# Fourteen pairs of up products instead of twelve in a two-layer hybrid decoder trunk

## The chip, the cores and the metric

The kernel runs on one core of one Trainium2 chip. The metric is the device time of one execution in microseconds (us); three executions are given by their median. Everything is float32 at the border; products on TensorE are made in three passes of a split format (below).

## The reference

Two layers, each with an RMS norm, one input projection, three kinds of mixing heads, an output projection, and an MLP. The change lies in the MLP alone:

```python
def rms_norm(x, g):
    y = x * lax.rsqrt(jnp.mean(x * x, axis=-1, keepdims=True) + NORM_EPS)
    return y * g
...
for l in range(DEPTH):                 # DEPTH = 2, SEQ = 512, D_MODEL = 1024, D_FF = 4096
    ...                                # mixing: x = x + mixed @ w_out[l]
    h = rms_norm(x, norm_mlp_g[l])
    x = x + jnp.square(jax.nn.relu(h @ w_mlp_up[l])) @ w_mlp_down[l]
return rms_norm(x, final_norm_g)
```

## The kernel before, in words

**Layout.** Everything is kept transposed: eight tiles `x[j]` of 128 features by 512 tokens. A weight group is 1024x128: eight blocks of 128x128, loaded as two halves of four blocks (256 KB each).

**Three passes.** Each product of a weight block and an activation block is three matmuls: high part by high part, high by low, low by high. So each weight half needs a cast to the high part on ScalarE (`whi`, L344) and a subtraction for the low part on VectorE (`wlo`, L345). The helper `weights()` hands out the halves from a ring of three buffers and one spare.

**The norm's factor late.** The up products take `x` times the norm weights (`acts`, tiles `ahif` and `alof`, eight each, L739 and L740); the factor of the norm per token (`rs`, tile `rsf`, copied at L771) is multiplied in afterwards, in `square()`: `r` = max(up, 0) times `rs` (VectorE, L1402), `m` = `r` squared (ScalarE, L1404), then `kept()` makes the split result `mh` (ScalarE, L1393) and `ml` (GpSimd, L1394), the "mids", in a ring of ten.

**Singles.** An up group made singly (`up(i)`) is 8 blocks x 3 passes = 24 matmuls of 512 columns. The first three (`NUP`) are issued in the hand-ordered stage of the layer (lists `ORDER`, run inside `manual_schedule`); the rest of the MLP is placed by the framework's scheduler, which gives each engine one fixed order.

**Pairs.** `two(i0, i1)` makes two up groups at once by a Strassen-Winograd scheme of 2x2 blocks: seven products (`p1` to `p7`) of four weight blocks each, 7 x 4 x 3 = 84 matmuls of 256 columns. It needs four sums of raw weights (`s1` to `s4`, VectorE, L1463), seven splits (`shi_p` on ScalarE L1457, `slo_p` on VectorE L1458), and, once for each layer, four kinds of block sums of the activations. Those are made in two steps: `bn[j]`, `x[j]` times the norm weights (ScalarE, L1429), which carries a bias `none` of zero whose only use is to order it after `rs`; and `blocks(k)`, which takes the pair `bn[k]`, `bn[k + 4]` and makes four half-width differences `t` (VectorE, L1435 to L1438), their high parts `thi` (ScalarE, L1442) and low parts `tlo` (VectorE, L1443). `p5`, `p6`, `p7` and `p4` each take one kind of sum of all four `k`. The tiles `bn[0..3]` and `bn[4..7]` share the two rings of five buffers (tags `shi`, `slo`) with the split sums of the pairs.

**Down.** `down(h, js)` adds to `x[j]` the product of the four mids 4h to 4h+3: 12 matmuls of 512 columns for each `j`, into one of two PSUM banks (tag `mm`), and one VectorE addition (L1518) that frees the bank.

**Order.** Eight singles, with `by_gain` and `blocks` issued after each of the last four; then `down(0)` for all eight `j`; then twelve pairs, each followed by half a down group as far as its mids are there. At the end of the second layer two pairs stand next to each other, and `last_group` makes the last down group and the final norm.

Of the kernel before, what the change touches and what calls it, by code (L numbers as in the profile page):

```python
# [10 lines left out]
F32 = mybir.dt.float32  # L11
# [12 lines left out]
P = 128  # L24
# [10 lines left out]
NG_IN = 26  # L35
# [140 lines left out]
         "wp/wlo 01201201201201202102102102102102102102102102102102102102102102102102102102 ")  # L176
NG = NG_IN + NG_OUT + NG_UP + NG_DN

N_ONE = 8

WHOLE = 5
PT = 1
# [86 lines left out]
def tile_trunk(ctx: ExitStack, tc: tile.TileContext, xT, wts, prm_d, cst_d, lora_d, gup_d, lam_d, fin_d, out):  # L269
# [299 lines left out]
    for l in range(L):  # L569
# [809 lines left out]
        with ExitStack() as mx:  # L1379
# [35 lines left out]

            bn, th = {}, {}
            none = cp.tile([P, NB], F32, tag="rr", bufs=2, name=f"none{l}")[:, :1]
            dve.tensor_scalar(none, rs[:, :1], 0.0, None, ALU.is_lt)  # L1420

            def by_gain(j):

                if j == 0:
                    fp.tile([P, 8], F32, tag="pad0", name=f"pad0_{l}")
                bn[j] = fp.tile([P, 2, H], F32, tag="shi" if j < 4 else "slo", bufs=5, name=f"bn{l}_{j}")
                if j == 4:
                    fp.tile([P, 24], F32, tag="pad1", name=f"pad1_{l}")
                act.activation(bn[j].rearrange("p a s -> p (a s)"), x[j], AF.Identity, scale=pr[:, C_GMLP + j:C_GMLP + j + 1],  # L1429
                               bias=none)  # L1430

            def blocks(k):
                b1, b2 = bn[k], bn[k + 4]
                t = [fp.tile([P, 2, H], F32, tag=f"s{2 * (k % 2) + i + 1}", name=f"t{l}_{k}_{i}") for i in range(2)]
                dve.tensor_tensor(t[0][:, 0], b1[:, 1], b1[:, 0], ALU.subtract)  # L1435
                dve.tensor_tensor(t[0][:, 1], b2[:, 1], t[0][:, 0], ALU.subtract)
                dve.tensor_tensor(t[1][:, 0], b2[:, 1], b1[:, 1], ALU.subtract)
                dve.tensor_tensor(t[1][:, 1], b2[:, 0], t[0][:, 1], ALU.subtract)  # L1438
                hi, lo = th[k] = [fp.tile([P, 4, H], F32R, tag=f"t{p}{k}", name=f"t{p}{l}_{k}") for p in ("hi", "lo")]
                for i in range(2):  # L1440
                    u = slice(2 * i, 2 * i + 2)
                    act.copy(hi[:, u], t[i])  # L1442
                    dve.tensor_tensor(lo[:, u], t[i], hi[:, u].bitcast(F32), ALU.subtract)  # L1443

            def two(i0, i1):

                n = f"{l}_{i0}"
                wg = wbase + NG_IN + NG_OUT

                def raw(i, a):  # L1450
                    t = fp.tile([P, 4, P], F32, tag="sraw", bufs=6, name=f"raw{n}_{i}_{a}")
                    nc.sync.dma_start(t.rearrange("p k c -> p (k c)"), wts[wg + i, :, a * P:(a + 4) * P])
                    return t

                def both(src, name):
                    hi, lo = [fp.tile([P, 4, P], F32R, tag=f"s{p}", bufs=5, name=f"s{p}{n}_{name}") for p in ("hi", "lo")]
                    act.copy(hi, src)  # L1457
                    dve.tensor_tensor(lo, src, hi.bitcast(F32), ALU.subtract)  # L1458
                    return hi, lo

                def sum_(name, a, b, op):
                    t = fp.tile([P, 4, P], F32, tag=name, name=f"{name}{n}")
                    dve.tensor_tensor(t, a, b, op)  # L1463
                    return t

                def small(name):
                    return fp.tile([P, H], F32, tag=name, bufs=2, name=f"{name}{n}")

                def product(pt, w, moving, first=True):

# [8 lines left out]
                smm = lambda q: lambda k: [p[:, q] for p in th[k]]  # L1479
# [24 lines left out]
                dve.tensor_tensor(c1, c1, p5, ALU.add)  # L1504
                s4 = sum_("s4", w12, s2, ALU.subtract)
                product(pb, both(s4, "p3"), blk(1, 1), False)
                dve.tensor_tensor(c0[:, H:], pb, u2, ALU.add)
                square([c0], f"{n}_0")
                product(pa, both(w22, "p4"), smm(3), False)
                square([pa, c1], f"{n}_1")  # L1510

            def down(h, js):

                g, k0 = h // 2, 4 * (h % 2)
                for j in js:
                    pt = psum("mm", 2, f"dn{l}_{h}_{j}")
                    mm3(pt, weights(wbase + NG_IN + NG_OUT + NG_UP + 8 * g + j, k0, k0 + 4), mids[4 * h:4 * h + 4], 4)
                    dve.tensor_tensor(x[j], pt, x[j], ALU.add)  # L1518
# [91 lines left out]
```

## Time and profile before

| what | value |
|---|---|
| median of 3 runs | 1241.13 us (1240.64 to 1241.17) |
| the profiled execution | 1241.0 us, its span 1239.2 us |
| TensorE matmul busy | 1227.2 us, 9572 matmuls |
| VectorE / ScalarE / GpSimd busy | 915.1 / 675.5 / 367.3 us |
| granted clock | 0.998 |

The span is the time from the first to the last instruction of the execution that was profiled. Busy times say how long an engine had at least one instruction in it; matmuls overlap (one of 512 columns shows 390 ns and the next starts 227 ns after it), so the pace of TensorE is read from the starts in the timeline and not from the durations. The first layer's MLP runs from about 279 us, the second layer's from about 889 us.

### The profile page before, as it was taken

How to read it: one execution, taken by the hardware profiler on the slowest of the kernel's cores; microseconds unless marked ns; L12 is line 12 of the kernel's file. 1: busy time of each engine (PE TensorE's matmuls, PEld its weight loads, DVE VectorE, ACT ScalarE, POOL GpSimd, SP SyncE). 2: the span in 40 equal slices, each digit the busy share in tenths (PEclk: the TensorE clock that was granted, in tenths of full speed). 3: DMA queues.
4: the chain of work that ended last, by engine and by line, in shares of the span. 5: the costliest groups of instructions: out<-in, count | busy, mean ns of one | idle time of the engine just before them, and what ended most of it. 6: DMA issues, size and time to landing. Idle time of an engine off the chain costs nothing.

```text
span 1239.2 us, 25134 instructions
## 1 busy us (share of the span) xinstructions
PE 1227.2 (99%) x9572; PEld 1050.8 (85%) x9572; DVE 915.1 (74%) x1776; ACT 675.5 (55%) x1410; POOL 367.3 (30%) x457
## 2 busy tenths in 40 slices
PE   9999999999999999999999999999999999999997
PEld 6788788888899998989888888888788999999987
DVE  6887888868767676765766777887686767676754
ACT  6785655548445454544565656564583545454543
POOL 2263637342311111120035454563231211111111
PEclk9999999999999999999999999999999999999999
DMA  6523333142433333321235243232433333323121
GB/s 216 164 88 98 108 92 111 53 154 85 136 102 96 108 95 103 102 85 44 69 104 167 82 131 111 88 84 71 152 103 121 101 102 102 103 95 109 53 68 69
DMA packets 84696, 127.92 MB, mean 103 GB/s; under 512 B 21472, under 2 KB 25568, under 8 KB 84576
## 3 DMA queue, kind: packets, MB, share of 16 engines
q1 hardware_dynamic: 83568, 125.64, 32.7%
q8 instruction: 75, 1.23, 0.4%
q10 hardware_dynamic: 1008, 0.68, 0.2%
q14 instruction: 45, 0.37, 0.1%
HBM read 117.11 MB, written 9.18 MB: 102 GB/s over the span
## 4 chain that ended last, share of the span: by engine, by line
PE 93%; DVE 2%; ACT 2%; POOL 1%; DMA 1%; issue 1%; ACTq 0%; POOLq 0%; DVEq 0%
PE dn L282 25%; PE pj L282 21%; PE pa L282 11%; PE po L282 8%; PE up L282 7%; PE pb L282 6%; PE dnF L282 4%; PE pc L282 3%; PE sc L282 1%; PE ptt L287 1%; PE pg L282 1%; DMA raw<-wts 1%; PE pyy L282 1%; PE pzw L282 1%; PE pst L282 1%
## 5 line engine op out<-in xcount | busy, mean ns | idle before, releaser
L1394 POOL TENSOR_TENSOR ml<-m,mh 128x512 fp32r<-128x512 f32 x64 | 108.9, 1716 | 480.9 <-ACT mh L1393 322.6
L344 ACT CAST whi<-raw 128x512 fp32r<-128x512 f32 x142 | 87.4, 619 | 162.1 <-PE dn L282 152.6
L282 PE MATMUL dn<-mh,whi 128*128 128x512 f32 x448 | 174.8, 390 | 0.0
L282 PE MATMUL dn<-ml,whi 128*128 128x512 f32 x448 | 174.6, 390 | 0.0
L282 PE MATMUL dn<-mh,wlo 128*128 128x512 f32 x448 | 174.5, 390 | 0.0
L683 POOL TENSOR_TENSOR wlo<-raw,whi 128x512 fp32r<-128x512 f32 x84 | 110.5, 1316 | 212.7 <-ACT whi L671 174.6
L282 PE MATMUL pj<-ahim,whi 128*128 128x512 f32 x392 | 156.8, 400 | 0.4 <-DVE vf L1280 0.4
L282 PE MATMUL pj<-ahim,wlo 128*128 128x512 f32 x392 | 156.5, 399 | 0.0
L282 PE MATMUL pj<-alom,whi 128*128 128x512 f32 x392 | 156.0, 398 | 0.0
L1518 DVE TENSOR_TENSOR x<-dn,x 128x512 f32<-128x512 f32 x112 | 77.3, 690 | 102.9 <-PE dn L282 102.9
L671 ACT CAST whi<-raw 128x512 fp32r<-128x512 f32 x142 | 87.7, 618 | 81.5 <-PE pj L282 27.6
L345 DVE TENSOR_TENSOR wlo<-raw,whi 128x512 fp32r<-128x512 f32 x142 | 115.2, 812 | 11.2 <-ACT whi L344 8.8
L282 PEld LDWEIGHTS dn<-mh,wlo 128*128 128x128 f32 x448 | 84.1, 188 | 17.8
L282 PEld LDWEIGHTS dn<-mh,whi 128*128 128x128 f32 x448 | 84.1, 188 | 17.5 <-issue 0.4
L282 PEld LDWEIGHTS dn<-ml,whi 128*128 128x128 f32 x448 | 84.1, 188 | 16.7
L1457 ACT CAST shi_p<-s 128x512 fp32r<-128x512 f32 x96 | 59.6, 621 | 70.0 <-PE pa L282 55.1
L282 PEld LDWEIGHTS pj<-ahim,whi 128*128 128x128 f32 x392 | 73.9, 188 | 14.1 <-issue 0.8
L282 PEld LDWEIGHTS pj<-alom,whi 128*128 128x128 f32 x392 | 73.9, 188 | 14.0 <-issue 0.5
L282 PEld LDWEIGHTS pj<-ahim,wlo 128*128 128x128 f32 x392 | 73.9, 188 | 13.9 <-issue 0.2
L1458 DVE TENSOR_TENSOR slo_p<-s,shi_p 128x512 fp32r<-128x512 f32 x96 | 68.0, 709 | 19.7 <-ACT shi_p L1457 17.2
L282 PE MATMUL pa<-tlo,shi_p 128*128 128x256 f32 x288 | 81.4, 282 | 0.0
L282 PE MATMUL pa<-thi,shi_p 128*128 128x256 f32 x288 | 81.2, 282 | 0.0
(414 smaller groups left out, 3202.4 us busy)
## 6 DMA issues: line engine op xcount, KB each, us to landing
raw<-wts SPq DMA_DIRECT2D x389, 256.0 KB, 2.7
qs<-dqhi SPq DMA_DIRECT2D x24, 128.0 KB, 3.7
ks<-dkhi SPq DMA_DIRECT2D x24, 128.0 KB, 3.7
x<-xT SPq DMA_DIRECT2D x8, 256.0 KB, 4.5
dqhi<-qhi SPq DMA_DIRECT2D x6, 256.0 KB, 3.3
dqlo<-qlo SPq DMA_DIRECT2D x6, 256.0 KB, 3.3
dkhi<-khi SPq DMA_DIRECT2D x6, 256.0 KB, 3.1
dklo<-klo SPq DMA_DIRECT2D x6, 256.0 KB, 3.5
```

The lines of the kernel that those rows point to most:

```text
L282: ins = nc.tensor.matmul(*a, **k)
L287: ins = nc.tensor.transpose(*a, **k)
L344: act.copy(hi[:, :n], raw[:, :n])
L345: (pool if a and lean[0] else dve).tensor_tensor(lo[:, :n], raw[:, :n], hi[:, :n].bitcast(F32), ALU.subtract)
L671: yield act.copy(hi[:, k0:k1], raw[:, k0:k1])
L683: yield eng.tensor_tensor(lo[:, k0:k1], raw[:, k0:k1], hi[:, k0:k1].bitcast(F32), ALU.subtract)
L1394: pool.tensor_tensor(lo, m, hi.bitcast(F32), ALU.subtract)
L1457: act.copy(hi, src)
L1458: dve.tensor_tensor(lo, src, hi.bitcast(F32), ALU.subtract)
L1518: dve.tensor_tensor(x[j], pt, x[j], ALU.add)
```

## The change

- Four up groups are made singly instead of eight (`N_ONE`), and fourteen pairs instead of twelve.
- `none` is made from the last low part of `acts` instead of `rs`, so that all `bn` depend on `x` and the norm weights only; the eight `by_gain` are issued together behind the four singles.
- `blocks` goes by kind of sum (`q`) and not by `k`: first the sums for `p5` of all `k`, then those for `p6`, `p7` and `p4`. The number of instructions is the same. It is issued behind the first half of `down(0)`.
- `down(0)` is made in two halves, the second behind the first pair. In the first, `j` = 0 and 1 open both banks together: three of the four mids for each, then the fourth for each.
- `s1` and `s3` of the first pair take `none` as an added scalar, and the copy of `p5` out of PSUM goes from VectorE to ScalarE.

```diff
-N_ONE = 8
+N_ONE = 4
...
-            dve.tensor_scalar(none, rs[:, :1], 0.0, None, ALU.is_lt)
+            dve.tensor_scalar(none, acts[NK - 1][1][:, :1].bitcast(F32), 0.0, None, ALU.mult)
...
-            def blocks(k):
-                b1, b2 = bn[k], bn[k + 4]
-                t = [fp.tile([P, 2, H], F32, tag=f"s{2 * (k % 2) + i + 1}", name=f"t{l}_{k}_{i}") for i in range(2)]
-                dve.tensor_tensor(t[0][:, 0], b1[:, 1], b1[:, 0], ALU.subtract)
-                dve.tensor_tensor(t[0][:, 1], b2[:, 1], t[0][:, 0], ALU.subtract)
-                dve.tensor_tensor(t[1][:, 0], b2[:, 1], b1[:, 1], ALU.subtract)
-                dve.tensor_tensor(t[1][:, 1], b2[:, 0], t[0][:, 1], ALU.subtract)
...
+            def blocks(q):
+                hi, lo = th[q] = [fp.tile([P, 4, H], F32R, tag=f"t{p}{q}", name=f"t{p}{l}_{q}") for p in ("hi", "lo")]
                 for i in range(2):
                     u = slice(2 * i, 2 * i + 2)
-                    act.copy(hi[:, u], t[i])
-                    dve.tensor_tensor(lo[:, u], t[i], hi[:, u].bitcast(F32), ALU.subtract)
+                    t = fp.tile([P, 2, H], F32, tag="c0" if q == 1 else ("s3", "s4")[i], bufs=1 + (q == 1), name=f"t{l}_{q}_{i}")
+                    for k in (2 * i, 2 * i + 1):
+                        b1, b2, o = bn[k], bn[k + 4], t[:, k % 2]
+                        if q == 0:
+                            dve.tensor_tensor(o, b1[:, 1], b1[:, 0], ALU.subtract)
+                        elif q == 1:
+                            dve.tensor_tensor(o, b2[:, 1], tb[0, i][:, k % 2], ALU.subtract)
+                        elif q == 2:
+                            dve.tensor_tensor(o, b2[:, 1], b1[:, 1], ALU.subtract)
+                        else:
+                            dve.tensor_tensor(o, b2[:, 0], tb[1, i][:, k % 2], ALU.subtract)
+                    tb[q, i] = t
+                    act.copy(hi[:, u], t)
+                    dve.tensor_tensor(lo[:, u], t, hi[:, u].bitcast(F32), ALU.subtract)
...
-                    dve.tensor_tensor(t, a, b, op)
+                    if i0 == N_ONE and name in ("s1", "s3"):
+                        dve.scalar_tensor_tensor(t, a, none, b, ALU.add, op)
+                    else:
+                        dve.tensor_tensor(t, a, b, op)
...
-                dve.tensor_copy(p5, pb)
+                act.copy(p5, pb)
...
             def down(h, js):
                 g, k0 = h // 2, 4 * (h % 2)
+                if h == 0 and js[0] == 0:
+                    pts = [psum("mm", 2, f"dn{l}_{h}_{j}") for j in js[:2]]
+                    ws = [list(weights(wbase + NG_IN + NG_OUT + NG_UP + 8 * g + j, k0, k0 + 4)) for j in js[:2]]
+                    for a, b in ((0, 3), (3, 4)):
+                        for j, pt, w in zip(js, pts, ws):
+                            for k in range(a, b):
+                                (whi, wlo), (ahi, alo) = w[k], mids[k]
+                                pe.matmul(pt, whi, ahi, start=(k == 0), stop=False)
+                                pe.matmul(pt, whi, alo, start=False, stop=False)
+                                pe.matmul(pt, wlo, ahi, start=False, stop=(k == 3))
+                    for j, pt in zip(js, pts):
+                        dve.tensor_tensor(x[j], pt, x[j], ALU.add)
+                    js = js[2:]
...
             for i in range(N_ONE):
                 up(i)
-                if i >= N_ONE - 4:
-                    k = i - N_ONE + 4
-                    by_gain(k)
-                    by_gain(k + 4)
-                    blocks(k)
-            down(0, range(NK))
-            h, half = 1, 0
+            for j in range(NK):
+                by_gain(j)
+            down(0, range(4))
+            for q in range(4):
+                blocks(q)
+            h, half = 0, 1
             for p in range(N_TWO):
                 two(N_ONE + p, N_ONE + N_TWO + p)
                 if len(mids) >= 4 * h + 6 and h < 2 * N_KG - 2 * (l == L - 1):
```

More of the change, by code (lines that the diff above doesn't have):

```diff
@@ L1414, in up @@
                 square([pt], f"{l}_{i}")
-            bn, th = {}, {}
+            bn, th, tb = {}, {}, {}
             none = cp.tile([P, NB], F32, tag="rr", bufs=2, name=f"none{l}")[:, :1]
-            dve.tensor_scalar(none, rs[:, :1], 0.0, None, ALU.is_lt)
+            dve.tensor_scalar(none, acts[NK - 1][1][:, :1].bitcast(F32), 0.0, None, ALU.mult)
             def by_gain(j):
@@ L1430, in by_gain @@
                                bias=none)
-            def blocks(k):
-                b1, b2 = bn[k], bn[k + 4]
-                t = [fp.tile([P, 2, H], F32, tag=f"s{2 * (k % 2) + i + 1}", name=f"t{l}_{k}_{i}") for i in range(2)]
[L1435 to L1439, printed above, removed]
+            def blocks(q):
+                hi, lo = th[q] = [fp.tile([P, 4, H], F32R, tag=f"t{p}{q}", name=f"t{p}{l}_{q}") for p in ("hi", "lo")]
                 for i in range(2):
                     u = slice(2 * i, 2 * i + 2)
-                    act.copy(hi[:, u], t[i])
-                    dve.tensor_tensor(lo[:, u], t[i], hi[:, u].bitcast(F32), ALU.subtract)
+                    t = fp.tile([P, 2, H], F32, tag="c0" if q == 1 else ("s3", "s4")[i], bufs=1 + (q == 1), name=f"t{l}_{q}_{i}")
[12 more added lines that the diff above has]
+                    dve.tensor_tensor(lo[:, u], t, hi[:, u].bitcast(F32), ALU.subtract)
             def two(i0, i1):
@@ L1478, in two @@
                 blk = lambda d, q: lambda k: [p[:, q * H:(q + 1) * H] for p in acts[4 * d + k]]
-                smm = lambda q: lambda k: [p[:, q] for p in th[k]]
+                smm = lambda q: lambda k: [p[:, k] for p in th[q]]
                 pa, pb = [psum("rp", 4, f"p{i}{n}")[:, :H] for i in "ab"]
```

## The prediction

> **What bounds the kernel now.** I read the page's busy times first, then what TensorE waited for, then its chain and its starts in the MLP, then a table of stages, and last the way of one up result to the mids.
>
> ```profile
> span 1239.2 us, 25134 instructions
> PE 1227.2 (99%) x9572; PEld 1050.8 (85%) x9572; DVE 915.1 (74%) x1776; ACT 675.5 (55%) x1410; POOL 367.3 (30%) x457
> PE idle L282 <- DVE zero L394: 1.2, 1, 1.2
> PE up L282 <- DVE alof L740: 0.6, 2, 0.3
> 289.27 35.62 PE up L282 x157
> 324.90 21.77 PE dn L282 x96
> ```
>
> TensorE is the bound. The longest of its waits is 1.2 us at the start; in the MLP only 0.6 us appear, twice 0.3. The chain of work that ended last runs through TensorE without a break from the singles (`up`) into the first down group (`dn`). So a saving counts only if it shortens TensorE's stream, and each new wait of TensorE counts in full. The pace comes from the starts:
>
> ```profile
> 302.75 0.39 PE L282 MATMUL up<-ahif,wlo 128*128 128x512 f32 x1
> 302.98 0.39 PE L282 MATMUL up<-ahif,whi 128*128 128x512 f32 x1
> ...
> 324.74 0.39 PE L282 MATMUL dn<-mh,whi 128*128 128x512 f32 x1
> ...
> 332.67 0.39 PE L282 MATMUL dn<-mh,wlo 128*128 128x512 f32 x1
> ...
> 346.50 0.28 PE L282 MATMUL pa<-ahif,shi_p 128*128 128x256 f32 x1
> ...
> 356.50 0.40 PE L282 MATMUL dn<-mh,whi 128*128 128x512 f32 x1
> ```
>
> Four singles of 24 matmuls lie between 302.98 and 324.74: 21.76 / 96 = 0.2267 us a matmul, 5.44 us a single. A pair lies between 346.50 and 356.50: 10.00 us. The stages say what fills them (columns: stage, its length, then busy time of PE, PEld, DVE, ACT, POOL, granted clock, DMA share, GB/s):
>
> ```profile
> 297.54:302.97 5.43, 5.43 (x25) 4.50 (x24) 5.39 (x12) 4.68 (x9) 1.23 (x1) 1.00 0.30 101
> 302.97:324.74 21.77, 21.77 (x98) 18.03 (x97) 21.71 (x34) 14.59 (x26) 10.10 (x4) 1.00 0.42 127
> 324.74:346.50 21.76, 21.76 (x97) 18.02 (x96) 12.19 (x17) 6.81 (x13) 2.58 (x2) 1.00 0.38 117
> 346.50:356.50 10.00, 10.00 (x85) 9.99 (x84) 8.17 (x15) 5.13 (x10) 0.00 (x0) 1.00 0.32 103
> 1163.98:1174.00 10.02, 10.02 (x86) 10.02 (x86) 7.58 (x14) 5.26 (x12) 0.00 (x0) 1.00 0.14 45
> 1174.00:1184.04 10.04, 10.04 (x85) 10.03 (x85) 6.34 (x12) 5.01 (x11) 2.60 (x2) 1.00 0.01 2
> ```
>
> Two things are to be seen. VectorE is full while the singles run (5.39 of 5.43, 21.71 of 21.77): the block sums are made there, and the first down group (12.19 of 21.76) is slack behind them. And a pair is a stream of weight loads without a gap (PEld 9.99 of 10.00), which is why it saves so little over two singles.
>
> **The change part by part.** *Four singles to two pairs, in each of two layers.* 8 x 5.44 - 4 x 10.00 = 43.5 - 40.0 = 3.5 us less on TensorE, all of it on the path. The Trainium skill ("TensorE: Matmul & The Clock Gate", section "Back-to-back issue gap") gives a gap of N / 2.4 + 2.5 ns between matmuls; as an estimate from that page a pair would be 84 x 0.109 = 9.2 us, a single 24 x 0.216 = 5.2 us, and the saving 4.8 us. The starts above give 3.5 us and decide.
>
> *Two pairs next to each other.* Behind the first pair's down half comes a pair with no down work after it. The last two rows of the table show such a couple in the second layer: 10.02 and 10.04 us, TensorE full. Cost nothing. If its cover went (splits prefetched five deep during the down half), VectorE's 8.17 of 10.00 would still fit.
>
> *`p5` copied by ScalarE* is one 256-wide copy in a stage where ScalarE is busy 5.13 of 10.00: nothing. *`s1` and `s3` as three-operand instructions*: `r` is one and takes 680 ns (row below), a plain sum 680 to 693: nothing.
>
> *`bn` ahead of the factor.* What it can win is seen at the seam:
>
> ```profile
> 283.57 1.41 DVE L740 SCALAR_TENSOR_TENSOR alof<-x,prm,ahif 128x512 fp32r<-128x512 f32 x2
> 285.71 0.62 ACT L671 CAST whi<-raw 128x512 fp32r<-128x512 f32 x1 [1.94 <-issue]
> 288.46 0.62 ACT L671 CAST whi<-raw 128x512 fp32r<-128x512 f32 x1 [2.13 <-PE up L282]
> 289.31 0.59 ACT L771 COPY rsf<-prbf 128x512 f32<-128x512 f32 x1 [0.23 <-PE prbf L282]
> 289.93 0.15 DVE L1420 TENSOR_SCALAR none<-rsf 128x1 f32<-128x1 f32 x1 [2.87 <-ACT rsf L771]
> ```
>
> The last `alof` is written by 284.98, `none` now follows it, and ScalarE has 1.94 + 2.13 us idle before 288.46, VectorE 2.87 us before 289.93. That is a head start of about 3 us for the block sums, no time of its own. A `bn` (0.81 us) may get ahead of the hand-ordered cast or of `rsf` and hold it that long; the next user is `r` of the first up group, for which TensorE does not wait. Nothing on the path.
>
> *The block sums lose their cover.* Before, they had until the first pair at 346.50. Now TensorE reaches the first pair after up group 3 (ends at 302.97) and four down groups, 48 x 0.2267 = 10.9 us: at 313.9, and `p5` 1.4 us later, at 315.3. What VectorE has to do from 290.0 until then goes by these groups of the stretch 290 to 346.5 (busy, mean ns | idle):
>
> ```profile
> L345 DVE TENSOR_TENSOR wlo<-raw,whi 128x512 fp32r<-128x512 f32 x20 | 16.0, 799 | 1.6 <-ACT whi L344 1.6
> L1429 ACT ACTIVATE bn<-x,none,prm 128x512 f32<-128x512 f32 x8 | 6.4, 809 | 0.2 <-DVE none L1420 0.2
> L1402 DVE SCALAR_TENSOR_TENSOR r<-up,rsf 128x512 f32<-128x512 f32 x8 | 5.4, 680 | 0.0
> L1443 DVE TENSOR_TENSOR tlo<-t,thi 128x512 fp32r<-128x512 f32 x8 | 5.3, 679 | 0.0
> L1435 DVE TENSOR_TENSOR t<-bn 128x256 f32<-128x256 f32 x4 | 2.8, 692 | 0.3 <-ACT bn L1429 0.3
> L1438 DVE TENSOR_TENSOR t<-bn,t 128x256 f32<-128x256 f32 x4 | 2.6, 659 | 0.0
> L1437 DVE TENSOR_TENSOR t<-bn,bn 128x256 f32<-128x256 f32 x4 | 2.4, 605 | 0.0
> L1458 DVE TENSOR_TENSOR slo_p<-s,shi_p 128x512 fp32r<-128x512 f32 x3 | 2.0, 679 | 0.0
> L1436 DVE TENSOR_TENSOR t<-bn,t 128x256 f32<-128x256 f32 x4 | 1.7, 416 | 0.8 <-ACT bn L1429 0.8
> ```
>
> Four `r` 2.7, six `wlo` (up group 3 and four down groups) 4.8, sixteen `t` 9.5, `tlo` of three kinds 4.1, two additions to `x` about 1.4, two weight sums and two `slo_p` 2.7: 25.2 us in 25.3, or in about 28 with the head start. All sixteen `t` count, because the splits of the first pair reuse the buffers that `bn` holds. It just fits; I take nothing for it, since the waits of the next part lengthen the window. Bounds 0 and, without the head start, about 1.5 us a layer (VectorE would have to fill every gap).
>
> *The first down half waits for mid 3.* This is new. Before, down group 0 began 21.76 us behind up group 3; now it comes directly behind it. The split into three mids and one puts 2 x 9 matmuls between: mid 3's `mh` is needed at 302.97 + 18 x 0.2267 = 307.05, its `ml` at 307.28. What the way from up group 3 to `ml` took before, first and second layer:
>
> ```profile
> 305.49 0.68 DVE L1402 SCALAR_TENSOR_TENSOR r<-up,rsf 128x512 f32<-128x512 f32 x1
> 306.27 0.63 ACT L1404 ACTIVATE m<-r 128x512 f32<-128x512 f32 x1
> 307.31 0.62 ACT L1393 CAST mh<-m 128x512 fp32r<-128x512 f32 x1
> 308.01 4.27 POOL L1394 TENSOR_TENSOR ml<-m,mh 128x512 fp32r<-128x512 f32 x1 [4.53 <-ACT mh L1393]
> ...
> 913.11 0.68 DVE L1402 SCALAR_TENSOR_TENSOR r<-up,rsf 128x512 f32<-128x512 f32 x1
> 915.81 1.74 POOL L1394 TENSOR_TENSOR ml<-m,mh 128x512 fp32r<-128x512 f32 x1 [4.37 <-ACT mh L1393]
> L1394 POOL TENSOR_TENSOR ml<-m,mh x64: 1288/1645/4512, 292.8 to 1186.6; 128x512 fp32r<-128x512 f32 x64
> ```
>
> Lower end: the bare durations, 303.14 (end of the matmul at 302.75) + 0.68 + 0.63 + 0.62 + 1.29 = 306.4, in time, 0. Upper end: the rows as they are, `ml` done at 312.28, 5.0 us late; in the second layer (up group 3 ended four singles before 932.65, at 910.9, `ml` needed at 915.2, done at 917.55) 2.35 us. I take `r` one VectorE instruction late (0.6) and the second layer's way from `r` to the end of `ml`, 917.55 - 913.11 = 4.44: 303.14 + 0.6 + 4.44 = 308.2, 0.9 us late in each layer. The lesser lateness of `r` is my choice: VectorE has fewer weight halves in hand here than during a row of singles. Queued behind the waiting matmuls on TensorE is everything else, the first pair too.
>
> *Both banks end together.* `j` = 2 needs the bank of `j` = 0, whose last matmul now starts only 4 x 0.2267 = 0.91 us before. The row below belongs to the matmul at 332.67 above: from there to the addition's end 333.79 - 332.67 = 1.12.
>
> ```profile
> 333.10 0.69 DVE L1518 TENSOR_TENSOR x<-dn,x 128x512 f32<-128x512 f32 x1 [1.13 <-PE dn L282]
> ```
>
> So 0.2 us of wait if VectorE is free, up to 0.8 if it is in another instruction; I take 0.3.
>
> **Sum.** The profiled execution took 1241.0 us, 0.1 under the median of 1241.13. -3.5 + 2 x (0.9 + 0.3) = -1.1: 1239.9 on that execution, 1240.0 against the median. About 0.2% (2.5 us) is what a measurement of this kernel can tell from no change, so this is "the same" by that bound.
>
> **The rivals.** *All of the saving stays.* `r` of group 3 meets a free VectorE, `ml` ends before 307.3 and the bank costs 0.2: 1241.13 - 3.5 + 0.4 = 1238.0. For it: the bare way has 0.9 us to spare and the head start takes load from VectorE. Against: `r` started 2.35 and 2.2 us after its product in the rows above.
>
> *`ml` is held, and the kernel gets slower.* Place: the GpSimd subtraction of mid 3. Its durations run from 1.29 to 4.51 us; the 4.27 row stands in the stretch where VectorE is full. With the old rows as they are the waits are 5.0 + 2.35, the banks 2 x 0.6: -3.5 + 8.55 = +5.0, 1246.1. It decides for slower once the waits pass 6.0 us in all, 3.0 a layer, `ml` later than about 7 us behind its product. Against: in the other row it took 1.74. The Trainium skill ("SBUF — State Buffer", section "SBUF: two separate sides") says that a two-input VectorE instruction and a GpSimd one take one port pair by turns, each for its whole length. By that rule the wait of `ml` is as long as VectorE's run of back-to-back subtractions; the 4.27 row agrees.
>
> *The head start doesn't come about*, because `bn` stays behind the hand-ordered `rsf` on ScalarE: then `p5` waits too, 1.5 us a layer: -1.1 + 3.0 = +1.9, 1243.0.
>
> **How the numbers follow.** Forecast 0.35 (1240.0, its own range 1238.7 to 1242), all of the saving 0.33 (1238.0), `ml` held 0.23 (1246.1), no head start 0.09 (1243.0). Faster by over 0.2% is the second, 0.33; slower the third, 0.23; the same 0.44. The low end lies just under the full saving with no wait at all, 1241.13 - 3.5 = 1237.6, less 0.3 for the runs; the high end takes in most of the third, 1245.8. No more than 2 in 10 is left out.
>
> **What would show it.** Matmuls: 96 fewer `up`, 168 more pair products in each layer. `bn` before `rsf` in ScalarE's order, or not. TensorE idle in front of `dn` for `ml`, within 6 us behind up group 3, about 0.9 us a layer; and once more for the addition to `x`. No idle in front of `pb` (`p5`). The prediction is wrong if TensorE's waits in the two MLPs sum to under 1 us or over 6, or if a pair is no longer 10.00 us.

## The result and the profile after

The changed kernel takes 1248.97 us in the median of 6 runs (1245.9 to 1249.9), the kernel before 1240.91 beside it: a ratio of 1.0064 (1.0051 to 1.0077). It is slower by 8 us, where 1240.0 was forecast and 1245.8 was the upper end. The profiled execution, 1245.9 us, happens to be the shortest of the six; a second series gave 1248.86 with a profiled execution of 1249.68. Five of the six runs lie between 1248.6 and 1249.9 us, so the longer profile is the usual execution. Both are shown, for the difference between them is part of the answer. First the page and the waits of TensorE of the shorter one (waits: us in total, times, longest):

```profile
span 1244.1 us, 25538 instructions
PE 1228.2 (99%) x9716; PEld 1055.9 (85%) x9716; DVE 931.8 (75%) x1796; ACT 693.0 (56%) x1462; POOL 363.6 (29%) x457
PE dn L282 <- DVE x L1535: 2.1, 2, 1.2
PE dn L282 <- POOL ml L1394: 2.0, 2, 1.0
PE prbf L282 <- POOL rrf L369: 0.6, 1, 0.6
```

and what has changed of these in the execution of 1249.68 us:

```profile
span 1247.9 us, 25538 instructions
PE dn L282 <- POOL ml L1394: 4.7, 2, 3.8
PE dn L282 <- DVE x L1535: 1.0, 1, 1.0
```

144 matmuls more are there (9716 for 9572, that is 168 - 96 in each layer), and there are three kinds of new wait: in the first down half for the `ml` of a mid and for the addition to `x`, and in the second layer for `prbf`, the broadcast of the norm's factor.

How much the first down half and the first pair lose is read from two starts: the first `dn` and the first matmul of the second pair. Between them lie 96 matmuls of 512 columns and one pair, 21.76 + 10.00 = 31.76 us by the prediction's pace. The shorter execution, first and second layer:

```profile
303.07 0.39 PE L282 MATMUL dn<-mh,whi 128*128 128x512 f32 x1
...
337.84 0.28 PE L282 MATMUL pa<-ahif,shi_p 128*128 128x256 f32 x1
...
914.54 0.39 PE L282 MATMUL dn<-mh,whi 128*128 128x512 f32 x1
...
948.98 0.28 PE L282 MATMUL pa<-ahif,shi_p 128*128 128x256 f32 x1
```

The longer one:

```profile
302.59 0.39 PE L282 MATMUL dn<-mh,whi 128*128 128x512 f32 x1
...
340.24 0.28 PE L282 MATMUL pa<-ahif,shi_p 128*128 128x256 f32 x1
...
917.79 0.39 PE L282 MATMUL dn<-mh,whi 128*128 128x512 f32 x1
...
952.13 0.28 PE L282 MATMUL pa<-ahif,shi_p 128*128 128x256 f32 x1
```

34.77 and 34.44 us, that is 3.0 and 2.7 too long; and 37.65 and 34.34, 5.9 and 2.6 too long. This *excess of the first stretch* serves below as the measure of each experiment. It is larger than the waits in it, in part since idle time is counted from the end of a matmul's record (0.39 us) and the pace from its start (0.2267 us). The prediction had 1.2 us a layer for it.

**Why `ml` comes late.** The same instruction, the fourth mid's `ml` of the first layer. Shorter execution:

```profile
304.92 0.68 DVE L1402 SCALAR_TENSOR_TENSOR r<-up,rsf 128x512 f32<-128x512 f32 x1
306.72 2.16 DVE L1446 TENSOR_TENSOR t<-bn,t 128x256 f32<-128x256 f32 x3
307.05 1.54 POOL L1394 TENSOR_TENSOR ml<-m,mh 128x512 fp32r<-128x512 f32 x1 [3.27 <-ACT mh L1393]
308.65 0.50 PE L282 MATMUL dn<-ml,whi 128*128 128x512 f32 x1 [1.04 <-POOL ml L1394]
...
311.94 0.50 PE L282 MATMUL dn<-mh,whi 128*128 128x512 f32 x1 [1.16 <-DVE x L1535]
```

Longer execution:

```profile
306.23 1.08 DVE L1446 TENSOR_TENSOR t<-bn,t 128x256 f32<-128x256 f32 x3
306.57 4.28 POOL L1394 TENSOR_TENSOR ml<-m,mh 128x512 fp32r<-128x512 f32 x1 [3.28 <-ACT mh L1393]
307.24 0.68 DVE L1464 TENSOR_TENSOR slo_p<-raw,shi_p 128x512 fp32r<-128x512 f32 x1
307.84 1.28 DVE L1449 TENSOR_TENSOR tlo<-t,thi 128x512 fp32r<-128x512 f32 x2
309.04 0.68 DVE L1464 TENSOR_TENSOR slo_p<-s,shi_p 128x512 fp32r<-128x512 f32 x1
310.90 0.50 PE L282 MATMUL dn<-ml,whi 128*128 128x512 f32 x1 [3.77 <-POOL ml L1394]
```

In both, `ml` starts 0.33 to 0.34 us after VectorE's three block sums do, that is, just as the second of them begins. In the shorter execution the second sum goes first, then `ml`, and the third sum is held: 1.49 us instead of 0.41. `ml` takes 1.54, against 1.29 when no sum runs beside it (the run with late sums below). Durations of the three sums, ns, lowest, median and highest:

```profile
L1446 DVE TENSOR_TENSOR t<-bn,t x3: 413/414/1489, 306.7 to 307.4; 128x256 f32<-128x256 f32 x3
```

In the longer one all three sums take 0.41, and `ml` stands through six VectorE instructions that follow each other, the last of which ends at 309.72; it ends 1.13 us after that. This is the prediction's rival "`ml` is held". The Trainium skill ("SBUF — State Buffer", section "SBUF: two separate sides") lets the loser wait out the winner's whole instruction. The held sum of the shorter execution agrees; in the longer one `ml` waited out a whole run of them. Nor is that the rule: the third mid's `ml`, a little earlier in the shorter execution, got in after some 1.5 us (2.80 - 1.29) with VectorE full, and held a `tlo` (1.77 instead of 0.68). What decides who goes first is not shown.

```profile
300.98 2.80 POOL L1394 TENSOR_TENSOR ml<-m,mh 128x512 fp32r<-128x512 f32 x1 [4.46 <-ACT mh L1393]
302.55 1.77 DVE L1449 TENSOR_TENSOR tlo<-t,thi 128x512 fp32r<-128x512 f32 x1
```

**The second layer waits for another mid.** The wait of 0.9 us for `ml` there comes, in both executions, at the eighth `dn` matmul, and that one takes the third mid. Shorter execution:

```profile
911.10 0.63 ACT L1404 ACTIVATE m<-r 128x512 f32<-128x512 f32 x1 [0.32 <-DVE r L1402]
911.75 1.28 ACT L474 ACT_TABLE_LOAD   x1
...
913.84 3.31 POOL L1394 TENSOR_TENSOR ml<-m,mh 128x512 fp32r<-128x512 f32 x1 [6.07 <-ACT mh L1393]
917.20 0.50 PE L282 MATMUL dn<-ml,whi 128*128 128x512 f32 x1 [0.92 <-POOL ml L1394]
```

A table load of 1.28 us, made on ScalarE for the square root of the final norm, stands between the third mid's `m` and its `mh`, and `ml` then takes 3.31 us. The fourth mid's `ml` (918.45 to 919.79) is not waited for.

**What a long wait adds.** The same stretch of the longer execution by windows (columns: window, its length, busy time of PE, PEld, DVE, ACT, POOL, granted clock, DMA share, GB/s):

```profile
308.00:312.00 4.00, 1.10 (x4) 0.92 (x5) 2.05 (x4) 0.56 (x1) 2.85 (x1) 0.97 0.00 0
312.00:314.00 2.00, 2.00 (x9) 1.85 (x8) 1.65 (x4) 0.67 (x2) 0.00 (x0) 0.50 0.00 0
314.00:316.00 2.00, 2.00 (x7) 1.58 (x7) 1.87 (x4) 0.62 (x1) 0.00 (x0) 0.70 0.00 0
316.00:318.00 2.00, 2.00 (x10) 1.63 (x9) 0.61 (x2) 0.62 (x1) 0.00 (x0) 1.00 0.82 229
```

After the wait TensorE works at half its clock: 4.00 x 0.03 + 2.00 x 0.50 + 2.00 x 0.30 = 1.7 us of pace lost in a stretch of 3.4 us. Nothing in the prediction provides for this.

### The profile page after: what moved, and what is told of

Its sections match the earlier page's. It is cut to its first block, busy times and chain, and to the rows that moved or that the text cites. A ratio compares the mean times of both kernels' runs of the same rounds, so it can differ in the third digit from the quotient of the medians.

```text
span 1244.1 us, 25538 instructions
## 1 busy us (share of the span) xinstructions
PE 1228.2 (99%) x9716; PEld 1055.9 (85%) x9716; DVE 931.8 (75%) x1796; ACT 693.0 (56%) x1462; POOL 363.6 (29%) x457
## 4 chain that ended last, share of the span: by engine, by line
PE 93%; DVE 3%; ACT 2%; DMA 1%; issue 1%; POOL 0%; POOLq 0%; SPq 0%; ACTq 0%; DVEq 0%
PE dn L282 24%; PE pj L282 22%; PE pa L282 13%; PE po L282 8%; PE pb L282 7%; PE dnF L282 4%; PE pc L282 3%; PE up L282 3%; PE sc L282 1%; PE ptt L287 1%; PE pg L282 1%; PE pyy L282 1%; DVE tlo L1449 1%; PE pzw L282 1%; PE pst L282 1%
## 5 line engine op out<-in xcount | busy, mean ns | idle before, releaser
L1394 POOL TENSOR_TENSOR ml<-m,mh 128x512 fp32r<-128x512 f32 x64 | 104.5, 1649 | 489.1 <-ACT mh L1393 348.0
L344 ACT CAST whi<-raw 128x512 fp32r<-128x512 f32 x126 | 77.7, 618 | 157.9 <-PE dn L282 148.1
L1540 DVE TENSOR_TENSOR x<-dn,x 128x512 f32<-128x512 f32 x108 | 74.5, 690 | 91.5 <-PE dn L282 91.3
L671 ACT CAST whi<-raw 128x512 fp32r<-128x512 f32 x142 | 87.7, 617 | 76.4 <-PE pj L282 28.9
L1463 ACT CAST shi_p<-s 128x512 fp32r<-128x512 f32 x112 | 69.5, 621 | 79.6 <-PE pa L282 62.3
L345 DVE TENSOR_TENSOR wlo<-raw,whi 128x512 fp32r<-128x512 f32 x126 | 100.2, 797 | 10.2 <-ACT whi L344 7.4
L282 PE MATMUL pa<-thi,shi_p 128*128 128x256 f32 x336 | 95.2, 283 | 0.1
L282 PE MATMUL pa<-tlo,shi_p 128*128 128x256 f32 x336 | 94.9, 282 | 0.0
L282 PE MATMUL pa<-thi,slo_p 128*128 128x256 f32 x336 | 94.2, 280 | 0.0
L1464 DVE TENSOR_TENSOR slo_p<-s,shi_p 128x512 fp32r<-128x512 f32 x112 | 77.7, 695 | 21.8 <-ACT shi_p L1463 19.0
```

What stands on the lines that cost most here:

```text
L282: ins = nc.tensor.matmul(*a, **k)
L344: act.copy(hi[:, :n], raw[:, :n])
L345: (pool if a and lean[0] else dve).tensor_tensor(lo[:, :n], raw[:, :n], hi[:, :n].bitcast(F32), ALU.subtract)
L671: yield act.copy(hi[:, k0:k1], raw[:, k0:k1])
L1394: pool.tensor_tensor(lo, m, hi.bitcast(F32), ALU.subtract)
```

## The experiments

The ratios are those to the kernel before on the same chip, with their intervals; "excess" is that of the first stretch, first / second layer, read from the two starts as above. The framework's scheduler lays out the order anew for each kernel, so a run can also move work that its edit does not name.

### The same kernel again

> The changed kernel once more, for a second profile. Theory W (TensorE's waits where the singles end): the profile shows the same four waits in front of the down matmuls, 1.0 to 1.2 us each, and every run lies near the profiled one, 1246. Theory C (clock): most runs lie near 1249 with a mean granted clock of 0.995 to 0.996 instead of 0.998, the waits in the records are the same as before, and the missing 3 us are a second stretch at half clock; if the profile falls on such a run, the stretch stands behind one of the waits, near 310 or 920 us.

1248.86 us, 1.0067 (1.0055 to 1.008). It is the longer execution shown above. Theory C is right on the time and the clock (0.996, one stretch at half); but the waits are not the same as before, as both theories had it. The excess of 5.9 in the first layer is the wait of 3.8, the clock's 1.7 and 0.4 of smaller gaps.

### The parts

```diff
 pairs_alone (the kernel before)
-N_ONE = 8
+N_ONE = 4
 late_none (the kernel after)
-            dve.tensor_scalar(none, acts[NK - 1][1][:, :1].bitcast(F32), 0.0, None, ALU.mult)
+            dve.tensor_scalar(none, rs[:, :1], 0.0, None, ALU.is_lt)
 no_halves (the kernel after)
-                if h == 0 and js[0] == 0:
+                if False:
 rest_alone (the kernel after)
-N_ONE = 4
+N_ONE = 8
```

The count alone:

> The kernel before with four singles instead of eight and nothing else. W: the first down group stands right behind up group 3 and needs the low part of mid 3 after nine or ten matmuls (2.2 us) where the old rows took 6.6 and 9.3 us, so TensorE waits 4 to 7 us in each layer: -3.5 + 8 to 14, so 1245.5 to 1251.5. C: one long wait instead of two short ones lowers the clock at least as often: clock 0.996 or less in most runs and 3 us more. Rival (the parts of the change other than the count cost the time): 1237.6 to 1241.

1257.94 us, 1.0137 (1.0121 to 1.0152). The waits of TensorE:

```profile
PE up L282 <- ACT whi L344: 5.5, 2, 4.1
PE pa L282 <- ACT p L1486: 3.3, 3, 1.4
PE dn L282 <- POOL ml L1394: 1.2, 2, 0.7
```

The count costs 17 us by itself, more than Theory W's range, and W had the place wrong: `ml` is waited for 1.2 us in all. The longest waits are for weight casts (`whi`), which stand behind `bn` and block copies in ScalarE's order, and stretches of 3.4 and 6.8 us at half the clock go with them (mean clock 0.993). So the rest of the change gives back 9 of the 17; I had not looked at ScalarE's queue.

Late gain copies:

> The changed kernel with the zero bias taken from the norm's factor again, so that the products of x and the norm weights start about 3 us later. W: VectorE and ScalarE have 3 us less, so the waits for ml and for the addition to x grow, by 1 to 3 us a layer: 1250 to 1254 (at the same clock 4 less). Rival (the head start disturbs the norm's chain and buys nothing): the wait of the factor's broadcast in the second layer (0.57 us) goes, the others stay, 0.5 to 1 us faster than the changed kernel.

1251.2 us, 1.0083 (1.0066 to 1.0099). The `prbf` wait is gone, `ml` is waited for 5.3 us, and a wait of 1.9 us for `p` comes in the third pair of the second layer. That is in Theory W's range. By the medians the head start is worth some 2 us, but the four runs spread from 1248.0 to 1254.2.

No halves:

> The changed kernel with the first down groups made one after the other. W: mid 3 is needed 2.04 us earlier, so its wait grows from 1.04 to about 3.1 us a layer, and the wait for the bank (1.16) goes: about +0.9 us a layer, 1.8 in all, 1250.8 or, in runs at clock 0.998, 1247.7. C: with one longer wait the clock falls at least as often. Rival (the opening of both banks costs more than it hides): no slower than the changed kernel.

1248.56 us, 1.0067 (1.0053 to 1.0081): the same as the kernel after, so the rival holds. Whole groups wait 1.5 and 1.8 us in the first layer, for the `mh` and the `ml` of the fourth mid, and lose the clock all the same. The wait for `x` is gone.

All the rest without the count:

> Eight singles and ten pairs as in the kernel before, with all the rest of the change (early gain copies, block sums by kind, first down group in halves). Theory A (the cost comes from having only four singles: 21.8 us of matmuls must then cover the gain copies, sixteen sums and the fourth mid): with 43.5 us of singles the sums are over before the eighth single ends, so no wait on `ml` over 0.5 us, no half clock; what stays is the `prbf` wait of 0.4 and at most 1.0 us for each layer at the third down group's PSUM bank: 1241 to 1243 us, granted clock as before. Theory B (the early copies and the sums by kind cost by themselves, in contention for the port and in the interleaved pair): 1245 us or more.

1241.91 us, 1.0006 (0.9996 to 1.0015), excess 0.3 / 0.3, no wait on `ml`: Theory A. With eight singles in front the rest costs next to nothing. It is the count that brings the waits.

### The mid, the sums and the clock

```diff
 ml_dve (the kernel after)
-                pool.tensor_tensor(lo, m, hi.bitcast(F32), ALU.subtract)
+                (dve if i == 3 else pool).tensor_tensor(lo, m, hi.bitcast(F32), ALU.subtract)
 late_sums (the kernel after): none made behind the singles
+            dve.tensor_scalar(none, mids[3][1][:, :1].bitcast(F32), 0.0, None, ALU.mult)
 fill (the kernel after), ahead of down(0, range(4))
+            if l == 0:
+                pt = psum("at", 2, "fill")
+                for i in range(12):
+                    pe.matmul(pt, mids[2][0][:, :P], mids[2][0], start=(i == 0), stop=(i == 11))
 head (the kernel after): two() yields behind p1 and p2 of the first pair
+            first = two(N_ONE, N_ONE + N_TWO)
+            next(first)
             down(0, range(4))
```

> As the kernel after, but the fourth mid's `ml` is made by VectorE instead of GpSimd, in both layers; by VectorE's order it stands behind most of the block sums. Theory H (GpSimd is kept out by VectorE's run of sums): the wait for `ml` in the first layer falls from 3.8 to 1.5 us or less, no half clock there, 1244 to 1246 us. Rival M (the chain r, m, mh itself, or VectorE's queue in front of `ml`, is as long): wait of 2.5 us or more and 1248 to 1250 us.

1243.55 us, 1.0021 (1.0011 to 1.003): 5.3 us less than the kernel after by one subtraction in each layer on another engine. The rows of the first layer:

```profile
306.77 0.68 DVE L1394 TENSOR_TENSOR ml<-m,mh 128x512 fp32r<-128x512 f32 x1
307.51 0.51 PE L282 MATMUL dn<-ml,whi 128*128 128x512 f32 x1 [0.18 <-DVE ml L1394]
```

`ml` takes 0.68 instead of 1.54 or 4.28, the wait falls from 3.8 to 0.2, and no half clock follows. Excess 1.9 / 1.5. Theory H holds, and M, that the chain itself is too long, does not. Not all of the 5.3 us is `ml`: in this kernel's order both additions to `x` also stand ahead of a `tlo`, and the wait for `x` is 0.5 us in the first layer and gone in the second.

> As the kernel after, but `none` is made from the fourth mid's `ml`, so that no gain copy and no block sum runs before that `ml` is done. Theory H (GpSimd's `ml` is kept from the SBUF by VectorE's run of sums, and the long wait then halves the clock): `ml` takes 1.6 us or less in both layers, the wait before the first down group is 0.6 to 1.3 us, no stretch of half clock, the `prbf` wait goes; with up to 1 us a layer at the third group's bank 1241 to 1243.5 us. Theory M (the fourth mid's own chain r, m, mh, ml is too long for the 4.1 us of matmuls in front of it, whatever the sums do): the wait stays at 2 us or more in each layer and the time at 1247 or more. Theory S (the sums now come too late for the first pair): waits of `pb` and `pa` on VectorE or ScalarE of 2 us or more in sum.

1254.18 us, 1.0107 (1.0091 to 1.0122). On `ml` H is right (1.29 us in both layers, no wait), yet Theory S decides:

```profile
PE pa L282 <- ACT p L1494: 3.0, 4, 1.3
PE dn L282 <- DVE x L1534: 2.0, 2, 1.1
PE pb L282 <- ACT shi_p L1462: 1.7, 2, 0.8
```

VectorE has no free room for the sums with four singles: moved out of the mid's way they stand in the first pair's, and ScalarE's copies (`p`) are late in the third.

> As the kernel after, with twelve matmuls of 128x512 more in the first layer between the fourth single and the first down group (the third mid's `mh` against itself into a PSUM bank that is free then and whose content nothing reads): 12 x 0.2267 = 2.7 us of work of no use. Theory C (an idle TensorE loses its clock, which costs a further 1.7 us): in the repetition of the kernel after the wait for `ml` was 3.8 us and a stretch of 3.4 us at half the clock followed; with the fill 2.7 of the 3.8 are covered by work, the wait is about 1.1 us, no half clock follows in the first layer, and the time is 1248.9 - 1.7 = 1247.2 us though more is computed. Rival N (the half clock has nothing to do with the wait): it stays, and the time is 1248.9 us. Rival T (the time of the fourth mid is not set by what runs beside it; everything is only moved): 1248.9 + 2.7 = 1251.6 us.

1248.85 us, 1.0065 (1.0051 to 1.0079): Rival N's number, 1.6 us above Theory C's. But it does not decide between them. In the profiled execution `ml` took 1.56 and was not waited for in the first layer; instead the third group waited 2.5 us for `x`, and a half clock followed that. The sum was the same with 2.7 us of useless work in it.

> As the kernel after, but the first pair's products p1 and p2, which need no block sum, are written ahead of the first down group; by the order of the program all 12 matmuls of p1 stand before the down group and p2's 12 are mixed into it. Theory F (the hole is only a lack of ready work between the fourth single and its mid): 12 x 0.119 = 1.4 us of the wait of 3.8 us in the first layer is filled, and the same in the second, the wait is then too short for the half clock in most runs: 1244 to 1246 us. Rival G (p1's weights are cast by ScalarE and VectorE, which are full with copies and sums just then, so p1 waits in its turn, and the mid comes later too): waits of the same sum, at `pa` instead of `dn`, and 1248 to 1250 us.

1245.17 us, 1.0034 (1.0021 to 1.0047): Theory F. No wait for `ml`, no half clock; 0.9 us of wait for `p` in the third pair of each layer are new.

### Six singles, and the wait for `x`

```diff
 six (the kernel before), six_rest, six_late, six_whole, six_whole_late, six_banks, six_banks_late (the kernel after)
+N_ONE = 6
 *_late: none from rs, as in late_none; *_whole*: `if False`, as in no_halves
 banks, six_banks*: the third and fourth down group of the first four mids
-                    pt = psum("mm", 2, f"dn{l}_{h}_{j}")
+                    pt = psum(*(("rp", 4) if h == 0 and j < 4 else ("mm", 2)), f"dn{l}_{h}_{j}")
 banks also: `ml` of mids 2 and 3 on VectorE
```

> The kernel before with six singles and thirteen pairs, nothing else changed. The count alone removes 4 x 0.2267 x 24 - 2 x 10.00 = 1.76 us over both layers. Theory A (32.6 us of singles still cover the gain copies and sums): no new wait, 1239.2 us. Rival L (each single that goes costs cover in proportion: with four singles the count alone ran 17.0 us longer): about half of that, 1247 to 1250 us.

1251.27 us, 1.0082 (1.0067 to 1.0097), worse than the rival's upper end: the first down group waits for `whi` (2.0 us, first layer) and `shi_p` (2.7 us, second) on ScalarE, and each wait is followed by half clock.

> As the kernel after, with six singles and thirteen pairs. Eight singles with the rest of the change gave 1241.9 us, four gave 1248.9. Theory A (a threshold: the fourth mid is the trouble, and with six singles the sums are over before the last single ends and mid 3 is long done): 1241.9 - 1.76 = 1240.1, plus the 0.8 us or so by which the down groups of the first layer run slower in every kernel with fewer singles: 1240 to 1241 us, no wait on `ml`. Rival L (each single that goes costs its cover): halfway, 1245.4 us.

1243.28 us, 1.002 (1.0012 to 1.0029), excess 2.1 / 2.1. No wait on `ml`, as Theory A said, but 1.8 and 1.7 us for `x`, which neither had.

> Six singles and thirteen pairs with block sums by kind and the first down group in halves, but the gain copies not made early (`none` from the norm's factor as in the kernel before). Theory A as for the kernel with the early copies: the `prbf` wait of 0.4 us in the second layer goes, no wait over 1 us comes in its place: 1239.5 to 1240.7 us, the best of all kernels so far if so. Rival: the copies are late for the first pair, as with four singles, where waits of 1.9 and 2.0 us at `pa` and `pc` came: 1242 us or more.

1248.86 us, 1.0066 (1.0053 to 1.0078). Theory A missed by 8 us: waits for `x` of 3.5 and 2.9 us, and 6.8 us at half the clock behind the second.

> As the kernel after (four singles), with the third and fourth mid's `ml` on VectorE and the third and fourth down groups in two PSUM banks that the singles have left, so that they wait for no eviction. With `ml` on VectorE for the fourth mid alone the time was 1243.55, with waits of 0.9 us (the third mid's `ml` on GpSimd, second layer) and about 0.5 and 1.0 us at the third group. Theory W (the waits add up one for one): 1243.55 - 0.9 - 0.5 to 1.0 = 1241.7 to 1242.2 us, and what is left above 1237.4 is the `prbf` wait, the down groups of the first layer, which run 1.8 us slower, and small waits at the first pair. Rival D (VectorE's queue is full, so its work only waits somewhere else: `slo`, `p` or `c` of the first pair): 1243 to 1244 us.

1241.49 us, 1.0004 (0.9995 to 1.0013), 0.2 below Theory W's range. Four singles, fourteen pairs, and the two waits taken away; the first stretch of the first layer is 32.22 us (302.43 to 334.65), 0.5 too long (second layer 0.9).

> Six singles and thirteen pairs, sums by kind, early gain copies; the first down group not in halves, each of its groups whole, with the first four mids long done. In halves this gave 1243.28 us, with 1.8 and 1.7 us of wait for `x` at the third group, since the first two groups end 0.7 us apart. Theory X (the halves make that wait): groups end 2.7 us apart, so `x` has 2 us more; the wait goes and the time is 1243.28 - 3.5 = 1239.8 us, faster than the kernel before by 0.1%. Rival D (`x` is late by VectorE's queue, whatever the spacing): 1242.5 us or more.

1245.22 us, 1.0041 (1.0028 to 1.0053): Rival D: with six singles and early copies `x` is late without the halves too. VectorE's rows and the waiting matmul:

```profile
318.10 1.28 DVE L1472 TENSOR_TENSOR s<-raw,raw 128x512 f32<-128x512 f32 x2
319.30 0.68 DVE L1472 TENSOR_TENSOR s<-s,raw 128x512 f32<-128x512 f32 x1
319.90 0.68 DVE L1540 TENSOR_TENSOR x<-dn,x 128x512 f32<-128x512 f32 x1
...
320.73 0.47 PE L282 MATMUL dn<-mh,whi 128*128 128x512 f32 x1 [2.00 <-DVE x L1540]
```

`x` starts the moment VectorE is done with sums that nobody needs yet; they stand ahead of it in its order. The run tells of the clock too. Here the wait of 2.0 us was followed by half clock, in both layers, and with six singles in halves 1.8 us was not; the excess is 3.9 / 3.9 against 2.1 / 2.1, and 1.8 us of difference is the clock's 1.7. In the two microseconds from 322 the granted clock is 0.50 here and 1.00 with halves.

> As the run with six singles and whole groups, but with late gain copies. In halves this gave 1248.86 us with waits for `x` of 3.5 and 2.9 us and 6.8 us at half the clock. Theory X: 1248.86 - 6.3 of waits - 3.4 of clock - 0.0 = 1239.2 us, as the `prbf` wait of 0.4 is gone too; about 1 us of the wait may stay, since 2 us of spacing do not cover 3.5: then 1240 to 1241. Rival D: 1245 us or more.

1243.17 us, 1.0017 (1.0009 to 1.0026), neither. The wait for `x` is gone, as Theory X had it; but one of 1.9 us for `shi_p` on ScalarE and one of 0.5 for `whi` have come. The 1.9 us were not followed by half clock.

> Six singles and thirteen pairs with all the rest of the change, and the third and fourth down groups of the first four mids in two PSUM banks that the singles have left. Theory W (only waits stand between the count and its saving): six singles gave 1243.28 us with 3.5 us of waits for `x`; these go: 1239.8 us, 0.1% below the kernel before. Rival D (work that is late on VectorE or ScalarE is then waited for at the first pair, which comes 3.5 us earlier: `shi`, `slo`, `p`, `tlo`): 1241.5 us or more.

1239.87 us, 0.9991 (0.9983 to 1.0), excess 0.05 / 0.06.

> The same with late gain copies. With the banks of the kernel after this gave 1248.86 us, with waits for `x` of 6.3 us and 6.8 us at half the clock. Theory W: 1248.86 - 6.3 - 3.4 = 1239.2 us. Rival D: the first pair waits for its block sums, which come later here than with early copies, 1242 us or more.

1239.3 us, 0.9988 (0.9979 to 0.9997): Theory W both times, 0.1 us from its figure. The stretch of the first layer is 31.81 us (313.36 to 345.17), that is, full pace; the second layer's is 0.4 too long. The list of TensorE's waits has none for `dn`, `pa`, `pb` or `pc`. The span is 1237.4 us.

This version beats both kernels: the one before by about 0.1%, which its interval just separates from nothing, and the one after by 0.8% (1239.3 against 1248.97).

## Why the prediction was wrong, point by point

- **The count, -3.5 us.** Right. The four singles that stay take 21.78 us less than eight did (24.05 from the first `up` to the first `dn` in the first layer, 45.83 before). With the waits away the saving shows, to within its other terms.
- **The first down half waits for mid 3, 0.9 us a layer.** This step failed, and with it the forecast. In the first layer the wait was 3.8 us in the usual execution and 1.0 in the shorter one; in the second the fourth mid was not waited for at all, and the 0.9 us there belong to the third mid, which the step does not have. So the figure is right there by luck.
  I let `r` start one VectorE instruction late (0.6); it came at 304.92, 1.85 us behind the first `dn` and so, as a product ends some 0.17 us behind the next start, 1.7 us after its product. From `r` to the start of `ml` it then took 2.1 us, where the row that I used has 2.7. And `ml` took 1.54 there, 0.2 less than I gave it. So the shorter execution comes out at 1.0, near the forecast, by errors that cancel for the most part.
  For `ml` I took the 1.74 us of the second layer's row and gave no reason; the fewer weight halves were my reason for `r` alone. But VectorE has the block sums in hand there, which the step before had just counted as filling it. In the usual execution `ml` took 4.28. The row of 4.27 us was the one to take: it stood in a stretch where VectorE was full, and so does the new place.
  The rival "`ml` is held" named this mechanism and should have had the larger chance. That its 1246.1 us lies nearer is partly luck: it held `ml` by 5.0 and 2.35 us in the two layers, where 3.8 and nothing came, and it has none of the terms below that made up for it.
- **The clock.** No term at all. 1.7 us for each half-clock stretch, one in the first layer in the usual execution.
- **Both banks end together, 0.3 us.** Mis-sized: 1.0 to 1.2 us where it shows. The bound of 0.8 counted one VectorE instruction ahead of `x`; the order has several. In the first layer of the shorter execution the product for `x` ends at 309.39:

```profile
309.40 1.28 DVE L1449 TENSOR_TENSOR tlo<-t,thi 128x512 fp32r<-128x512 f32 x2
310.61 0.68 DVE L1464 TENSOR_TENSOR slo_p<-s,shi_p 128x512 fp32r<-128x512 f32 x1
311.21 1.27 DVE L1535 TENSOR_TENSOR x<-dn,x 128x512 f32<-128x512 f32 x2
```

  The halves have a part in it, but not the whole: with whole groups the wait was gone with four singles, and with six singles and late copies, but stayed at 2.0 us with six and early copies.
- **`bn` ahead of the factor, "nothing on the path".** Nearly right in the first layer, where four copies (from 286.36) did go ahead of `rsf`, which starts at 289.71 instead of 289.31. In the second layer they brought the `prbf` wait of 0.6 us, for `rrf` on GpSimd; the singles there take 0.45 us longer for it. With late copies that wait shrinks or goes.
- **Two pairs next to each other, 0.** 0.5 us too small in each layer: the second and third pair, from 337.84 to the row at 358.33 below, take 20.49 us instead of 20.00. The stream stops twice in the third pair, for 0.3 and 0.2 us. Each time a product that adds onto `pa` starts just after ScalarE's copy out of `pa` (the first is `p1`), and in ScalarE's order that copy stands behind the `mh` and `m` of the pair before:

```profile
350.55 0.63 ACT L1404 ACTIVATE m<-r 128x512 f32<-128x512 f32 x1
351.09 0.35 ACT L1495 COPY p<-pa 128x256 f32<-128x256 f32 x1
351.49 0.39 PE L282 MATMUL pa<-thi,shi_p 128*128 128x256 f32 x1
```

  The prediction went by how full TensorE was in such a couple, and left out ScalarE's order in it. The longer waits for `p` in the runs above stand at the first of these two places.
- **The block sums lose their cover, 0.** Right as to `p5`, no wait over 0.3 us stands before `pb`. Wrong as to what the full VectorE does to others: `ml` and `x` are its victims, not the sums' own user.
- **A slower down half, unforeseen and unexplained.** Eleven periods, each a pair and a down half, lie between these rows of the first layer (shorter execution):

```profile
358.33 0.40 PE L282 MATMUL dn<-mh,whi 128*128 128x512 f32 x1
...
589.77 0.40 PE L282 MATMUL dn<-mh,whi 128*128 128x512 f32 x1
```

  231.44 / 11 = 21.04 us in the first layer; in the second it is 188.34 / 9 = 20.93 (969.46 to 1157.80), which is also the pace before. Over some twelve periods that is 1.3 us. All kernels with four singles have it, and `six`; the other kernels with six have not. What makes some twenty of the 48 matmuls there about 6 ns slower stays open.

The usual execution adds up so: -3.5 for the count, 5.9 + 2.6 for the first stretch, 0.45 for `prbf`, 1.0 for the couples of pairs, 1.3 for the slow down halves: +7.7, of 8.7 us by which its span is longer (1247.9 against 1239.2). About 1 us lies outside these. Some 0.8 of it lies between the layers, from the last `dn` of the first to the first `up` of the second: 267.91 us, against 267.10 before. Why is open. For the shorter one the same sum is -3.5 + 3.0 + 2.7 + 0.45 + 1.0 + 1.3 = +4.9, and its span is 4.9 us longer; for `banks` -3.5 + 0.5 + 0.9 + 0.45 + 1.0 + 1.3 = +0.7, with 0.6 measured.

So the saving was real, and it was taken back, first by VectorE's order and by GpSimd's `ml` being held beside a full VectorE, with the clock on top: that follows from the runs that move one subtraction (5.3 us) and then take the bank away (2.1 us, with a second subtraction moved). Even then the kernel only draws level with the one before. The 0.45, 1.0 and 1.3 us stay, the last of them unexplained.

## What to carry to other kernels

When work on the bounding engine is shortened, ask what the neighbours made in its shadow, and look through the order of each full engine for small instructions on the path (a split, an eviction) that stand behind bulk work which nobody needs yet; a duration measured beside a full engine is the one to take. A GpSimd subtraction beside a full VectorE took from 1.5 to 4.3 us here, and if something waits for it, VectorE's own 0.7 us are cheaper although VectorE is the fuller engine. A free PSUM bank can be worth more than a better order: with six singles it let late evictions be late at no cost, and gave 3.4 us.

## What was not expected of the hardware

- A wait of TensorE of 2 to 4 us is often, but not always, followed by a stretch at half the clock, mostly of 3.4 us, 1.7 us lost (twice it was 6.8 us). After 3.8, 2.7, 2.5 and 2.0 us it was; after single waits of 1.8 and 1.9 us, once after 2.4 us (four singles, late copies, second layer) and once after 3.5 us (six singles, late copies, first layer) it was not. Two waits of 1.5 and 1.8 us close to each other (no halves) were enough. The Trainium skill ("TensorE: Matmul & The Clock Gate", section "Part 1: The HAM clock gate") has a free-running window of 3413 ns and a fall to half after an idle window of about that length. The length of the stretch agrees, and that the fall doesn't depend on the wait's length alone fits a window that runs free; but 2.0 us of idleness were enough here, less than the page's window.
- GpSimd is not sure of a turn between two VectorE instructions that follow each other: in the longer execution `ml` stood for some 3 us (306.57 to 309.72) while six of them ran; in the shorter one it got in behind the first of them, and the next one waited for it.
